# A decoder step on one core: the experts' lists of the first 256 tokens completed in three parts, one input-projection block to a head, and a number table made at the start

## The chip, the cores and the metric

The kernel runs on one core of one Trainium2 chip. The metric is the device time of one execution in microseconds (us), the median of several runs. The core has a matmul engine (PE), three engines for element-wise work (DVE, ACT, POOL), an engine that here only issues transfers (SP), and 16 DMA engines. POOL issues the indirect transfers, which fetch rows of a table by a list of numbers.

## The reference, cut to what matters

One layer is computed for 512 prompt tokens and 8 samples (one new token each), width 1024: a norm, an input projection, attention and retention, an output projection, a second norm, and then a mixer of single-neuron experts:

```
def _peer_block(xb, w_pq, sub_keys, peer_u, peer_v):
    q = (xb @ w_pq).reshape(blk, PEER_HEADS, 2, PEER_HALF)
    s = jnp.einsum('thcd,hcnd->thcn', q, sub_keys).astype(jnp.float32)
    sv, si = lax.top_k(s, PEER_TOPK)
    ...
    best, pos = lax.top_k(cand, PEER_TOPK)
    eid = jnp.take_along_axis(cidx, pos, -1)
    g = jax.nn.softmax(best, -1).astype(xb.dtype)
    u = peer_u[eid]
    a = jax.nn.gelu(jnp.einsum('thkd,td->thk', u, xb))
    return jnp.einsum('thk,thkd->td', g * a, peer_v[eid])
```

Each token has 8 heads. A head scores 2 x 128 keys, keeps the 16 best of each half, and of their sums the 16 best again. These are 16 of 16,384 experts, each a row of 1024 numbers in `peer_u` and one in `peer_v`. The layer ends in a last norm.

## The kernel before, in words

The prompt is worked on in two waves of 256 tokens, A and B; B also carries the samples. Wave A goes through attention, retention, output projection and second norm first. Then `product_keys(0, ...)` makes its lists. Head by head it projects the tokens with two blocks of `w_pq` (`project`), multiplies the result with the keys (`psco`, L846), copies the scores out of PSUM on ACT (`sc`, L850), and finds the 16 best of each half on DVE (`tk_axis`, `top16`). After each fourth head `tk_finish` completes the lists of four heads: 80 candidate sums, their 16 best, the experts' numbers `eidL` (L351) and the gates.

Between two heads runs `second`, a generator of wave B's input projection in 28 blocks of 128 columns, with B's attention and retention between them; `BLOCKS` of these blocks are done for each head.

The two waves meet the experts in different ways. Wave A and the samples *gather*. For each head and each of its 16 places, POOL issues one indirect transfer (`gather`, L929) of 128 rows of `peer_u` (128 x 1024 numbers), DVE makes the dot product (L947), and after 16 of these come 16 gathers of `peer_v` that DVE weighs and adds up (`y`, L961). There are 528 gathers: 256 for tokens 0 to 127 (`lists[0]`), 256 for tokens 128 to 255, 16 for the samples. They share 8 buffers (`GBUFS`). Wave B is *dense*: all 16,384 experts are computed for its tokens, 128 at a time, in 128 blocks ("keys"): `dense_a` (L1065, eight matmuls with a block of the turned `peer_u`), `dense_w` (L1180, times a weight that is zero for an expert not chosen) and `dense_y` (L1187, four matmuls with a block of `peer_v` that SP loads, `vt`, L1174). The weights are made by `scatter` from B's lists: it compares the lists with a table of numbers (`iota128`, `iotaE`) and multiplies on PE (L1155 to L1168). `scatter(0, n)`, 32 groups, runs ahead of the dense loop, `scatter(1, n)` inside it.

The gathers are threaded through the rest of the program by hand: `beside(g, n, per)` takes `per` gathers after each step of `g`. The numbers are in `STEPS`:

```
STEPS = (16, 7, 5, 2)
...
    step[0] += STEPS[0]
    run(work, STEPS[0])
    beside(second, 28, STEPS[1])
    inB.close()
    beside(outer(1, (catB,), hnD, None), 8, STEPS[2])
```

16 are taken at once when wave A's lists are written, 7 after each block of `second` that is left (12 of them), 5 after each of the 8 blocks of wave B's output projection (`outer(1, ...)`, which ends in the second norm and so in `hnD`, L807), 2 after each head of wave B's `product_keys(1, ...)`: 156 in all. 16 more are taken in `scatter(0)`, the others at an even pace in the dense loop and behind it. While wave B's lists are made, PE also gets `dense_a` of the first keys (`paF`).

This written order goes through a scheduler, which orders the instructions by a simulated time line; the result is one fixed queue for each engine. Each engine runs its queue in order and stands at the first instruction whose inputs are not there.

Of the kernel before, what the change touches and what calls it, by code (L numbers as in the profile page):

```python
# [9 lines left out]
F32 = mybir.dt.float32  # L10
F32R = mybir.dt.float32r
BF16 = mybir.dt.bfloat16
# [21 lines left out]
DT = 512 - GT  # L34
# [6 lines left out]
LASTA = False  # L41
CHUNKS = [0, 64, 128]
ROWS = max(b - a for a, b in zip(CHUNKS, CHUNKS[1:]))
NG = DT // 8
STEPS = (16, 7, 5, 2)
BLOCKS = 2
SOON, RATE = 16, 574
AHEAD0 = 14

# [2 lines left out]
def step_kernel(ctx, tc, x_prompt, x_sample, cache_k, cache_v, state_ret, norm1_g, w_in, ret_gn_g,  # L52
                w_out, norm2_g, w_pq, sub_keys, peer_u, peer_v, norm_f_g, u_turned, keys_turned,
                y_p, y_s, kw_p, vw_p, ret_p, kn_s, vn_s, ret_s):
    nc = tc.nc
# [8 lines left out]
    consts = ctx.enter_context(tc.tile_pool(name="consts", bufs=1))  # L64
# [24 lines left out]
    su = setup.enter_context(tc.tile_pool(name="su", bufs=1, side="right"))  # L89

    def f_iota(pool, name, p, n, pattern, base, cm):
        t = pool.tile([p, n], F32, name=name)
        nc.gpsimd.iota(t, pattern=pattern, base=base, channel_multiplier=cm,
                       allow_small_or_imprecise_dtypes=True)
        return t
# [4 lines left out]
    def ps_tile(tag, name):  # L100
        return ps.tile([128, 512], F32, name=name, tag=tag, bufs={"o": 1, "x": 1}.get(tag, 2))
# [88 lines left out]
    selT = consts.tile([128, 8], F32, name="selT")  # L190
    iota16 = consts.tile([128, TOPK], BF16, name="iota16")
    nc.vector.tensor_copy(iota16, f_iota(su, "iota16f", 128, TOPK, [[1, TOPK]], 0, 0))

    bias = fc.tile([128, 512], F32, name="bias")
    mult = fc.tile([128, 512], F32, name="mult")
# [43 lines left out]
    def tk_new(pool, name, p, heads, eid):  # L239
        d = {"p": p, "H": heads, "n": name}  # L240
        if eid:
            d["g"] = pool.tile([128, heads, TOPK], F32, name=f"g{name}")
            d["eid"] = pool.tile([128, heads, TOPK], I32, name=f"eid{name}")
        return d

    def tk_open(pool, d):
        tag = d["tmp"] + str(d["H"])
        d["val"] = pool.tile([128, d["H"], 2, TOPK], F32, name="val" + d["n"], tag="val" + tag, bufs=1)
        d["idx"] = pool.tile([128, d["H"], 2, TOPK], U32, name="idx" + d["n"], tag="idx" + tag, bufs=1)

    def lockstep(gens):

        gens = list(gens)
        while gens:
            gens = [g for g in gens if next(g, gens) is not gens]
# [13 lines left out]
    def tk_axis(pool, d, h, c, src, key):  # L269
        p = d["p"]  # L270
        return top16(pool, d["val"][:p, h, c, :], d["idx"][:p, h, c, :], src, p, NKEY, key)
# [213 lines left out]
    def retention(w, h, rqT, rkT, kdN, rvN):  # L485
# [28 lines left out]
        for T in range(2):  # L514
            cs = slice(T * 128, (T + 1) * 128)
            nc.tensor.matmul(po[:, cs], inn[:, cs], rvN[:, T, :], start=True, stop=(before[T] is None))
            if before[T] is not None:
# [9 lines left out]
                   allow_small_or_imprecise_dtypes=True)  # L527
# [296 lines left out]
    def product_keys(w, lists, listS, hn):  # L824
        qst = ExitStack()
        qp = qst.enter_context(tc.tile_pool(name="qp", bufs=2, side="right"))
        n = hn.shape[2]
        if w:
            pss = ps_tile("x", "pss")
        for d in lists:  # L830
            tk_open(qp, d)
        for hc, pas in project(w_pq2, [(hn,)], range(16)):
            hh, c = divmod(hc, 2)
            if c == 0:
                qT = qp.tile([128, 2, WT + 8], F32, name="qT")
            nc.scalar.activation(qT[:, c, :n], pas[0][:, :n], AF.Copy)  # L836
            if c == 0:
                continue
            if w:
                for c in range(2):  # L840
                    nc.tensor.matmul(pss[:, c * 64 + hh * 8:c * 64 + hh * 8 + 8], keysT[:, 2 * hh + c, :],
                                     qT[:, c, WT:], start=True, stop=True)
            pc = ps_tile("s", "psco")
            for j in range(2):
                for c in range(2):
                    nc.tensor.matmul(pc[:, (2 * j + c) * 128:(2 * j + c + 1) * 128],  # L846
                                     qT[:, c, j * 128:(j + 1) * 128], keysT[:, 2 * hh + c, :],
                                     start=True, stop=True)
            sc = qp.tile([128, 4, 128], F32, name="sc", tag="sc", bufs=SCB)
            nc.scalar.activation(sc.rearrange("p a b -> p (a b)"), pc, AF.Copy)  # L850
            lockstep(tk_axis(qp, lists[j], hh, c, sc[:, 2 * j + c, :], 2 * j + c) for j in range(2) for c in range(2))
            if hh % 4 == 3:
                lockstep(tk_finish(qp, d, hh - 3, hh + 1, LASTA or hh < 4) for d in lists)
            yield
        if w:
            sst = qp.tile([128, 128], F32, name="sst", bufs=1)
            nc.scalar.activation(sst, pss[:, :128], AF.Copy)
            psr = ps_tile("s", "psr")
            for c in range(2):
                nc.tensor.transpose(psr[:64, c * 128:(c + 1) * 128], sst[:, c * 64:(c + 1) * 64], ident)  # L860
            tk_open(qp, listS)
            ssc = qp.tile([64, 2, 128], F32, name="ssc", bufs=1)
            nc.scalar.activation(ssc.rearrange("p a b -> p (a b)"), psr[:64, :256], AF.Copy)
            lockstep(tk_axis(qp, listS, 0, c, ssc[:, c, :], c) for c in range(2))
            lockstep([tk_finish(qp, listS, 0, 1)])
            for q in range(2):
                for nm in ("eid", "g"):
                    nc.sync.dma_start(wideS[nm][q * 64:(q + 1) * 64, 0, :],
                                      listS[nm][:64, 0, q * TOPK // 2:(q + 1) * TOPK // 2])
        qst.close()  # L870


    lists = [tk_new(pD, f"L{b}", 128, PH, b < 2) for b in range(4)]
# [30 lines left out]
    def outer(w, c2, hn, outs):  # L904

        ost = ExitStack()
        op_ = ost.enter_context(tc.tile_pool(name="op", bufs=1, side="right"))
        x = op_.tile([128, 2, D], F32, name="xo")
        xs = op_.tile([8, D], F32, name="xs") if w else None
        load_x(w, x, xs)  # L910
        ssq2 = small.tile([128, 3, KB], F32, name="ssq2", tag="ssq2", bufs=1)
        nc.vector.memset(ssq2, 1.0)
        yield from out_proj(op_, c2, x, xs, ssq2)
        norm2(op_, w, x, xs, ssq2, hn)
        ost.close()
# [108 lines left out]
    def beside(g, n, per, more=None):  # L1024

        for _ in g:
            step[0] += per
            run(work, per)
            if more is not None:
                more()  # L1030

    def run(g, n=1):
        for _ in range(n):
            if g is not None:
                next(g, None)
# [8 lines left out]
    for _ in product_keys(0, lists[:2], None, hnA):  # L1044
        run(second, BLOCKS)
    nc.vector.tensor_copy(catB[:, :, WT:], catS)
# [5 lines that stand above are left out]
    mixB.close()  # L1052
# [38 lines left out]
    def early():  # L1091
        h = head[0]
        head[0] += 1
        run(first, 2 * (AHEAD0 * (h + 1) // PH - AHEAD0 * h // PH))

    beside(product_keys(1, lists[2:], listS, hnD), 8, STEPS[3], early)
    EARLY = step[0]
    front.close()

    den = ExitStack()  # L1100
    dn = den.enter_context(tc.tile_pool(name="dn", bufs=1, side="right"))
    dw = den.enter_context(tc.tile_pool(name="dw", bufs=2, side="right"))
# [2 lines left out]
    pgs = [pY.tile([128, 512], F32, name=f"pg{q}") for q in range(2)]  # L1105
    paT, pgt = ring[0], pgs[0]
    yps = [[pY.tile([128, 512], F32, name=f"y{b}{q}") for q in range(2)] for b in range(2)]
    iota128f = dw.tile([128, DT], F32, name="iota128f", tag="lgt")[:, :128]
    nc.gpsimd.iota(iota128f, pattern=[[1, 128]], base=0, channel_multiplier=0, allow_small_or_imprecise_dtypes=True)
    iota128 = dn.tile([128, 128, 8], BF16, name="iota128")  # L1110
    nc.vector.tensor_copy(iota128, iota128f[:, :, None].to_broadcast([128, 128, 8]))

    iotaE = dn.tile([128, 16, 8], BF16, name="iotaE")
    nc.vector.tensor_copy(iotaE, iota128f.rearrange("p (a b) -> p a b", b=8))

    l5 = dn.tile([128, 5, DT], BF16, name="l5")
    lJ, lI, lg3 = l5[:, 0], l5[:, 1], l5[:, 2:]
# [187 lines left out]
```

## Time and profile before

| what | value |
|---|---|
| median of 3 runs | 1716.3 us (1715.61 to 1717.32) |
| profiled execution, its own time | 1717.34 us |
| span of the profile | 1715.6 us |
| PE busy | 1522.8 us, 89% |
| DVE busy | 1188.2 us, 69% |
| POOL busy | 772.7 us, 45% |
| ACT busy | 415.7 us, 24% |
| moved by DMA | 507.14 MB |

The profiled execution's own time is 1.7 us above the span: what lies outside the first and the last instruction. Durations below are of this one execution. "Busy" leaves out register, semaphore and DMA-issuing instructions. PE shows two records for each of these f32 matmuls.

### The profile page before, as it was taken

What the parts mean: (1) busy time and instruction counts of PE and PEld (TensorE: products, weight loads), DVE (VectorE), ACT (ScalarE), POOL (GpSimd) and SP (SyncE); (2) the same over time, 40 slices, a digit from 0 to 9 for tenths busy, and PEclk for the clock granted to TensorE, in tenths of its full rate; (3) what the DMA queues carried; (4) which work ended last, traced back from release to release, by engine and by line L of the source; (5) the groups of instructions that cost most, each with busy time, mean ns of one, the idle gap of its engine ahead of it and who ended that gap; (6) DMA issues with size and microseconds to landing.
All of it is one profiled execution on the core that took longest, in us unless ns stands there. A gap on an engine that the chain in (4) does not pass through costs nothing.

```text
span 1715.6 us, 21739 instructions
## 1 busy us (share of the span) xinstructions
PE 1522.8 (89%) x7544; PEld 1117.8 (65%) x7544; DVE 1188.2 (69%) x2869; ACT 415.7 (24%) x846; POOL 772.7 (45%) x656
## 2 busy tenths in 40 slices
PE   5987789998764698996799999999999999999995
PEld 5975647876653487886566667667676666666642
DVE  5667614597998699979997666566556555555666
ACT  5743623342212311326411112111110000000001
POOL 2155330035567674105764544444454544544552
PEclk9988899998886799995699999999999999999998
DMA  6577674379999999553599989999998999999996
GB/s 197 154 205 221 196 213 143 107 234 361 325 350 362 344 364 350 172 197 102 173 405 405 355 325 367 332 334 343 344 339 333 392 357 372 353 358 360 332 409 238
DMA packets 213517, 507.14 MB, mean 296 GB/s; under 512 B 16552, under 2 KB 103128, under 8 KB 213280
## 3 DMA queue, kind: packets, MB, share of 16 engines
q0 software_dynamic: 81952, 295.80, 47.2%
q1 hardware_dynamic: 131456, 209.95, 35.5%
q8 instruction: 60, 0.98, 0.2%
q14 instruction: 49, 0.40, 0.1%
HBM read 495.82 MB, written 9.86 MB: 295 GB/s over the span
## 4 chain that ended last, share of the span: by engine, by line
PE 32%; issue 26%; DVE 16%; POOL 10%; DMA 7%; ACT 2%; POOLq 0%; SPq 0%; DVEq 0%; ACTq 0%
PE pa L1065 8%; PE y L1187 8%; PE pa L157 8%; POOL v L929 5%; POOL u L929 4%; DVE y L961 3%; DVE u L947 3%; PE pg L1166 2%; DMA v<-in_peer_v,eidL 2%; DMA raw<-in_w_out 2%; DVE oi L1160 1%; DMA raw<-in_w_pq 1%; DMA kv<-in_cache_v_win 1%; DVE oj L1155 1%; PE paF L1065 1%
## 5 line engine op out<-in xcount | busy, mean ns | idle before, releaser
L929 POOL DMA_INDIRECT u<-in_peer_u,eidL x256 | 331.5, 1295 | 379.6 <-PE pT L452 113.2
L929 POOL DMA_INDIRECT v<-in_peer_v,eidL x256 | 331.2, 1294 | 303.4 <-DVE a L947 123.0
L1187 PE MATMUL y<-vt,ge 128*128 128x512 f32 x1024 | 460.5, 596 | 7.5 <-DVE y L961 7.5
L1065 PE MATMUL pa<-hnD,ut 128*128 128x256 f32 x1792 | 410.2, 382 | 4.8 <-ACT ge L1069 4.8
L1065 PEld LDWEIGHTS pa<-hnD,ut 128*128 128x128 f32 x1792 | 340.6, 192 | 81.5 <-issue 34.9
L961 DVE SCALAR_TENSOR_TENSOR y<-v,gw,y 128x1024 f32<-128x1024 f32 x261 | 336.1, 1288 | 19.8 <-DMA v<-in_peer_v,eidL 11.2
L1187 PEld LDWEIGHTS y<-vt,ge 128*128 128x128 f32 x1024 | 195.6, 191 | 209.8 <-issue 203.7
L947 DVE CUSTOM_DVE_ANT_0 u<-u,hq 128x1024 f32<-128x1024 f32 x264 | 313.6, 1217 | 9.0 <-DMA u<-in_peer_u,eidL 9.0
L1180 DVE TENSOR_TENSOR ge<-ge,big 128x256 f32<-128x256 f32 x128 | 52.0, 423 | 197.3 <-ACT ge L1069 183.4
L1069 ACT ACTIVATE ge<-pa 128x256 f32<-128x256 f32 x112 | 42.9, 383 | 502.8 <-PE pa L1065 400.8
L157 PE MATMUL pa<-hnD,raw 128*128 128x256 f32 (+1 forms) x512 | 128.3, 403 | 10.6 <-DMA raw<-in_w_pq 8.1
L1166 PEld LDWEIGHTS <-oj 128*128 128x128 bf16 x1536 | 100.1, 167 | 42.5 <-DVE oi L1160 25.4
L157 PEld LDWEIGHTS pa<-hnD,raw 128*128 128x128 f32 x512 | 101.2, 202 | 35.7 <-issue 11.2
L1155 DVE TENSOR_TENSOR oj<-iota,l 128x1024 bf16<-128x1024 bf16 x64 | 44.0, 687 | 100.8 <-PE pg L1166 92.0
L157 PE MATMUL pa<-xTB,raw 128*128 128x256 f32 x448 | 106.1, 390 | 1.3 <-DMA raw<-in_w_in 1.3
L157 PEld LDWEIGHTS pa<-xTB,raw 128*128 128x128 f32 x448 | 85.5, 197 | 14.1 <-ACT qT L836 0.9
L1168 ACT ACTIVATE big<-pg 128x512 f32<-128x512 f32 x48 | 53.2, 1109 | 152.5 <-PE pg L1166 130.9
L1166 PE MATMUL pg<-oi,oj 128*128 128x64 bf16 x1152 | 75.9, 230 | 14.7 <-DVE oi L1160 13.6
L126 PE MATMUL pa<-xT,wh 128*128 128x264 f32 x224 | 70.4, 315 | 8.7 <-ACT xT L119 4.4
L127 PE MATMUL pa<-xT,wh 128*128 128x264 f32 x224 | 68.3, 305 | 0.1
L128 PE MATMUL pa<-xT,wl 128*128 128x264 f32 x224 | 67.6, 302 | 0.6 <-DVE wl L120 0.6
L1160 DVE TENSOR_TENSOR oi<-oi,lx 128x1536 bf16<-128x1536 bf16 x64 | 60.3, 950 | 0.0
(515 smaller groups left out, 1720.4 us busy)
## 6 DMA issues: line engine op xcount, KB each, us to landing
ut<-in_u_turned SPq DMA_DIRECT2D x128, 512.0 KB
vt<-in_peer_v SPq DMA_DIRECT2D x128, 512.0 KB
raw<-in_w_in SPq DMA_DIRECT2D x56, 512.0 KB
raw<-in_w_pq SPq DMA_DIRECT2D x16, 1024.0 KB
raw<-in_w_out SPq DMA_DIRECT2D x8, 1024.0 KB
kv<-in_cache_k_win POOLq DMA_DIRECT2D x24, 256.0 KB
kv<-in_cache_v_win POOLq DMA_DIRECT2D x24, 256.0 KB
u<-in_peer_u,eidL POOLq DMA_INDIRECT x256
```

Source lines behind the costliest of these rows:

```text
L126: nc.tensor.matmul(out, wh, xh, start=first, stop=False)
L127: nc.tensor.matmul(out, wh, xl, start=False, stop=False)
L128: nc.tensor.matmul(out, wl, xh, start=False, stop=last)
L157: nc.tensor.matmul(pa[:, :n], part[:, k, :], x[0][:, k, :], start=(k == 0), stop=(k == KB - 1))
L929: nc.gpsimd.indirect_dma_start(out=t[:p], out_offset=None, in_=tab, in_offset=bass.IndirectOffsetOnAxis(ap=d["eid"][:p, h, k:k + 1], axis=0))
L947: nc.vector.tensor_tensor_reduce(out=u[:p], in0=u[:p], in1=hn, scale=1.0, scalar=0.0, op0=OP.mult, op1=OP.add, accum_out=a[:, k:k + 1])
L961: nc.vector.scalar_tensor_tensor(y, v[:p], w[:, k:k + 1], y, op0=OP.mult, op1=OP.add)
L1065: nc.tensor.matmul(pa, ut[:, k, :], hnD[:, k, :DT], start=(k == 0), stop=(k == KB - 1))
L1155: nc.vector.tensor_tensor(out=oj, in0=iota128, in1=lJ[:, None, ts].to_broadcast([128, 128, 8]), op=OP.is_equal)
L1160: marks[c] = nc.vector.tensor_tensor(out=oi3, in0=oi[:, None].to_broadcast([128, 3, ne, 64]), in1=lx[:, 1:, None].to_broadcast([128, 3, ne ...
L1166: nc.tensor.matmul(pg_[:, t * ni:(t + 1) * ni], oj[:, :, t], oi3[:, z, :, es], start=(z == 0), stop=(z == 2))
L1187: nc.tensor.matmul(yps[b][q], ge[:, b * 128:(b + 1) * 128], vt[:, q * 512:(q + 1) * 512], start=(i == 0), stop=(i == NKEY - 1))
```

## The change

Four things change. `STEPS` and `BLOCKS`: one block of `second` to a head in place of two, so that 20 blocks are left behind wave A's lists in place of 12, with 5 gathers to a block in place of 7; ahead of `product_keys(1)`'s end stand 16 + 100 + 40 + 16 = 172 gathers in place of 156. `ENDS`: the lists of wave A are completed after heads 1, 3 and 7 (heads 0 and 1, 2 and 3, 4 to 7) in place of 3 and 7; those of wave B as before. The number table: 128 numbers in bf16 are made among the constants, and the den stage copies from them.

```
-STEPS = (16, 7, 5, 2)
-BLOCKS = 2
+STEPS = (16, 5, 5, 2)
+BLOCKS = 1
+ENDS = ((1, 3, 7), (3, 7))
...
+    iota128b = consts.tile([128, 128], BF16, name="iota128b")
+    nc.vector.tensor_copy(iota128b, f_iota(su, "iota128f", 128, 128, [[1, 128]], 0, 0))
...
-            if hh % 4 == 3:
-                lockstep(tk_finish(qp, d, hh - 3, hh + 1, LASTA or hh < 4) for d in lists)
+            if hh in ENDS[w]:
+                h0 = max([0] + [e + 1 for e in ENDS[w] if e < hh])
+                lockstep(tk_finish(qp, d, h0, hh + 1, LASTA or hh < 4) for d in lists)
...
-    iota128f = dw.tile([128, DT], F32, name="iota128f", tag="lgt")[:, :128]
-    nc.gpsimd.iota(iota128f, pattern=[[1, 128]], base=0, channel_multiplier=0, allow_small_or_imprecise_dtypes=True)
     iota128 = dn.tile([128, 128, 8], BF16, name="iota128")
-    nc.vector.tensor_copy(iota128, iota128f[:, :, None].to_broadcast([128, 128, 8]))
-
-    iotaE = dn.tile([128, 16, 8], BF16, name="iotaE")
-    nc.vector.tensor_copy(iotaE, iota128f.rearrange("p (a b) -> p a b", b=8))
+    nc.vector.tensor_copy(iota128, iota128b[:, :, None].to_broadcast([128, 128, 8]))
+
+    iotaE = iota128b.rearrange("p (a b) -> p a b", b=8)
```

The scheduler makes new queues of this. Three places follow; in the changed kernel the line numbers are 3 to 4 higher up to the den stage and 1 higher behind it.

DVE's queue before, at the first dot product (L947). `eidL_296` and `eidL_298` are the experts' numbers of the first and second 128 tokens, and 128x64 is four heads of 16:

```order
L345 TENSOR_TENSOR pick_3430<-eq 128x64
L343 TENSOR_TENSOR eq<-eq 128x64x8
L351 SCALAR_TENSOR_TENSOR eidL_296<-pick_3410,pick_3430 128x64
...
L351 SCALAR_TENSOR_TENSOR eidL_298<-pick_3412,pick_3432 128x64
L448 RECIPROCAL rs<-sm 128x1
L947 ISA u,a<-u,hq 128x1024
L947 ISA a 128x1
L258 MAX valL_2807<-sc 128x8 x2
```

The same place of the changed kernel; 128x32 is two heads of 16:

```order
L354 SCALAR_TENSOR_TENSOR eidL_300<-pick_3021,pick_3041 128x32
L261 MAX valL_2811<-sc 128x8 x2
L261 MAX valL_2813<-sc 128x8 x2
...
L354 SCALAR_TENSOR_TENSOR eidL_302<-pick_3023,pick_3043 128x32
L444 ISA lg,nm<-psc,bh 128x384
L444 ISA nm 128x1
L269 MAX_INDEX idxL_2812<-valL_2811,rest 128x8
L951 ISA u,a<-u,hq 128x1024
```

The first dot product stood behind the lists of heads 0 to 3; it now stands behind those of heads 0 and 1. From there to the rows that write `hnD` at the end of wave B's second norm, DVE's queue held 108 to 110 dots and sums, and now holds 152 to 154. The two completions of wave A's lists held 198 DVE instructions, the three now hold 254.

PE's queue before, at the last heads of wave B's lists (`pa<-hnD,raw` is the projection with `w_pq`, `paF` is `dense_a` of the first keys, `psco` a head's scores):

```order
L157 MATMUL pa<-hnD,raw 128x264 x16
L1065 MATMUL paF<-hnD,ut 128x256 x16
L841 MATMUL pss<-qT,keysT 128x8 x2
L846 MATMUL psco<-keysT,qT 128x128
L1065 MATMUL paF<-hnD,ut 128x256 x8
L846 MATMUL psco<-keysT,qT 128x128 x3
L860 MATMUL psr<-ident,sst 64x128 x2
L1065 MATMUL paF<-hnD,ut 128x256 x48
```

The same place of the changed kernel:

```order
L1069 MATMUL paF<-hnD,ut 128x256 x15
L158 MATMUL pa<-hnD,raw 128x264 x16
L1069 MATMUL paF<-hnD,ut 128x256 x3
L844 MATMUL pss<-qT,keysT 128x8
L849 MATMUL psco<-keysT,qT 128x128
L1069 MATMUL paF<-hnD,ut 128x256 x6
L844 MATMUL pss<-qT,keysT 128x8
L849 MATMUL psco<-keysT,qT 128x128 x3
L1069 MATMUL paF<-hnD,ut 128x256 x7
```

Ahead of the last head's first `psco` PE's queue held 64 `paF` matmuls between the heads, and now holds 105. In `scatter(0)` it held groups of 21, 12 and 4 `dense_a` matmuls between the scatter's own, and now holds none there; the dense loop behind it is unchanged. On DVE, the stretch of wave B's lists held 45 dots and sums, and now holds 17.

SP's queue before, at the program's end (`hx` is the rows to which the samples' sum is added, `xb` those of wave B):

```order
L1174 DMA vt<-in_peer_v 128x1024 x15
L966 DMA hx<-hs 8x1024
L982 DMA out<-y 128x1024
L1174 DMA vt<-in_peer_v 128x1024 x5
L1253 DMA xb<-hs 128x1024 x2
L982 DMA out<-y 8x1024
L1269 DMA out<-xb 128x512 x4
```

The same place of the changed kernel:

```order
L1175 DMA vt<-in_peer_v 128x1024 x10
L970 DMA hx<-hs 8x1024
L986 DMA out<-y 128x1024
L1175 DMA vt<-in_peer_v 128x1024 x6
L1254 DMA xb<-hs 128x1024 x2
L1175 DMA vt<-in_peer_v 128x1024
L986 DMA out<-y 8x1024
L1175 DMA vt<-in_peer_v 128x1024 x3
L1270 DMA out<-xb 128x512 x4
```

The load of `hx` stood five `vt` loads before the last one, and now stands ten before it. PE's matmul that adds up the samples (`selT`, two halves) stood one key before the end of PE's queue, and now stands eight keys before it. Behind DVE's last `dense_w` stood 42 gathers, and now stand 27. On POOL, the `iota` of the den stage stood behind the first 163 gathers and is gone there.

## Rows read from the trace of the kernel before

**Rows 1.** Stretches: busy us of each engine, granted PE clock, DMA share, GB/s.

```profile
300.00:364.00 64.00, 64.00 (x347) 52.41 (x346) 44.97 (x257) 28.09 (x60) 0.00 (x0) 1.00 0.41 117
364.00:598.00 234.00, 156.94 (x726) 126.43 (x725) 196.88 (x531) 57.45 (x141) 147.96 (x117) 0.82 0.97 345
598.00:706.00 108.00, 102.03 (x475) 87.85 (x475) 105.50 (x407) 23.66 (x49) 60.20 (x48) 0.94 0.92 332
706.00:746.00 40.00, 35.22 (x157) 30.36 (x156) 37.77 (x216) 11.32 (x23) 0.00 (x0) 0.91 0.37 119
746.00:842.00 96.00, 72.38 (x895) 67.89 (x893) 85.34 (x144) 51.01 (x79) 50.52 (x17) 0.67 0.45 149
842.00:1620.00 778.00, 778.00 (x3285) 527.85 (x3283) 484.78 (x709) 93.53 (x182) 385.95 (x316) 1.00 0.95 355
1620.00:1716.00 96.00, 76.62 (x173) 32.57 (x171) 65.64 (x82) 11.18 (x22) 39.80 (x34) 0.92 0.82 322
```

**Rows 2.** Timeline of DVE: at the first gather, and at wave B's second norm.

```profile
363.02 0.21 DVE L351 SCALAR_TENSOR_TENSOR eidL<-pick,pick 128x64 int32<-128x64 f32 x1
368.91 1.25 DVE L947 CUSTOM_DVE_ANT_0 u<-u,hq 128x1024 f32<-128x1024 f32 x1 [3.31 <-DMA u<-in_peer_u,eidL]
...
601.00 0.86 DVE L807 TENSOR_SCALAR hnD<-pt,gT 128x256 f32<-128x256 f32 x2
```

**Rows 3.** Timeline of ACT: scores of wave A's heads 1 and 3, wave B's head 7.

```profile
287.66 0.58 ACT L850 ACTIVATE sc<-psco 128x512 f32<-128x512 f32 x1
329.65 0.59 ACT L850 ACTIVATE sc<-psco 128x512 f32<-128x512 f32 x1
707.27 0.60 ACT L850 ACTIVATE sc<-psco 128x512 f32<-128x512 f32 x1 [0.28 <-PE psco L846]
```

**Rows 4.** Timeline of POOL: the first gather, and the number table.

```profile
364.18 1.08 POOL L929 DMA_INDIRECT u<-in_peer_u,eidL  x1 [113.16 <-PE pT L452]
747.42 0.24 POOL L1109 IOTA iota128f<- 128x128 f32 x1 [50.61 <-DVE eidS L351]
```

**Rows 5.** DMA queues, 300 to 364 us: packets, MB, share of 16 engines.

```profile
q1 hardware_dynamic: 11058, 7.44, 40.3%
```

**Rows 6.** DMA queues, 364 to 598 us.

```profile
q0 software_dynamic: 16248, 59.20, 68.0%
q1 hardware_dynamic: 26798, 21.46, 29.1%
```

**Rows 7.** DVE's groups by shape, 364 to 598 us: busy, mean ns, idle before.

```profile
L947 DVE CUSTOM_DVE_ANT_0 u<-u,hq 128x1024 f32<-128x1024 f32 x64 | 76.7, 1216 | 6.8 <-DMA u<-in_peer_u,eidL 6.8
L961 DVE SCALAR_TENSOR_TENSOR y<-v,gw,y 128x1024 f32<-128x1024 f32 x45 | 59.4, 1320 | 0.3
L947 DVE DVE_READ_ACCUMULATOR2_ANT a<- 128x1 f32 x64 | 5.0, 79 | 0.0
```

**Rows 8.** A stretch of the dense loop, columns as in the first group.

```profile
875.00:900.00 25.00, 25.00 (x116) 16.73 (x115) 22.41 (x29) 3.20 (x7) 18.28 (x15) 1.00 1.03 409
```

**Rows 9.** PE's groups by shape, 598 to 706 us.

```profile
L1065 PE MATMUL paF<-hnD,ut 128*128 128x256 f32 x127 | 28.9, 379 | 0.0
```

**Rows 10.** Timeline of DVE: the number table and the scatter.

```profile
747.69 0.69 DVE L1111 CAST iota<-iota128f 128x1024 bf16<-128x1024 f32 x1 [0.43 <-POOL iota128f L1109]
751.87 0.69 DVE L1155 TENSOR_TENSOR oj<-iota,l 128x1024 bf16<-128x1024 bf16 x1 [3.35 <-ACT l L1125]
762.06 0.69 DVE L1155 TENSOR_TENSOR oj<-iota,l 128x1024 bf16<-128x1024 bf16 x1 [2.51 <-PE pg L1166]
770.18 0.69 DVE L1155 TENSOR_TENSOR oj<-iota,l 128x1024 bf16<-128x1024 bf16 x1 [3.22 <-PE y L1166]
```

**Rows 11.** Timelines of DVE, PE and SP's queue at the program's end.

```profile
1693.35 1.28 DVE L961 SCALAR_TENSOR_TENSOR y<-v,gw,y 128x1024 f32<-128x1024 f32 x1 [0.43 <-DMA v<-in_peer_v,eidW]
1682.51 16.21 PE L1187 MATMUL y<-vt,ge 128*128 128x512 f32 x32 [7.54 <-DVE y L961]
1673.05 0.29 SPq L966 DMA_DIRECT2D hx<-hs  x1
```

## The prediction

> **What bounds the kernel now.** I read the stretches first, cut where the work changes [rows 1]. From 300 to 364 us PE is busy throughout, at the full granted clock: wave A's lists with blocks of wave B's input projection between them. From 364 to 598 us PE works 157 of 234 us, and the DMA engines are at 97% with 345 GB/s: gathers, and wave B's weights. Up to 706 us PE is the bound again (102 of 108), with DVE full beside it (105.5). From 706 to 746 us DVE completes wave B's lists, to 842 us it makes the scatter (85 of 96), and from there to 1620 us PE is busy without a gap at full clock. Behind that come 96 us in which the gathers that are left end.
>
> Then I looked for what opens each stretch. Wave A's head 3 has its scores on ACT at 329.65 us [rows 3], DVE writes the experts' numbers of heads 0 to 3 at 363.02, POOL issues the first gather at 364.18 [rows 4], and DVE makes the first dot product at 368.91 after 3.31 us of waiting for the transfer [rows 2]. The stretch that follows ends when DVE has written `hnD` (601.00 us the last row of it), because everything from PE's `product_keys(1)` on needs that. DVE's queue is in order, so `hnD` cannot be written before the dots and sums that stand ahead of it, and those not before their rows have landed.
>
> **The change part by part.** *First gather.* The lists now start with heads 0 and 1. Head 1's scores come at 287.66 us, and about 284 without one of the two blocks that stood ahead of them. Behind the scores of head 3 stand 34 us to the first gather, for four heads' completion; for two I take two thirds, 22. The gathers start near 305 us in place of 364.
>
> *Front end.* This is the large term. Ahead of `hnD` 152 to 154 gathers must now be consumed where it was 108 to 110: 45 more, against a start that is 59 us earlier. What a gather costs: 59.20 MB of the indirect queue [rows 6] are 113 landed gathers of 0.524 MB. So some 157 must land, 82.3 MB, and beside them what the hardware queue moved from 300 us on, 7.44 MB [rows 5] and 21.46 MB [rows 6], and 1 MB that I add for what is cut off at the ends: 112.2 MB. At the 345 GB/s that this mix had with the engines full, that is 325 us: from 305 to 630. The other way, by the engines' own time: a gather took 0.68 of 234 us over 113, 1.41 us, so 157 take 221; the loads took 68.1 us (29.1% of 234), 25.8 us (40.3% of 64) and some 3 us for the added 1 MB. That is 318 us, at 97% 328: 633. DVE sets the other bound. A dot with its read-out, or a sum, costs (76.7 + 5.0 + 59.4) / 109 = 1.29 us [rows 7]; 154 of them make 199 us, the other work of DVE in the two stretches was 45.0 + 55.8, and 56 more instructions for the third completion cost 0.2 us each by the 128x64 row at 363.02 [rows 2], 11 us. Together 311: not before 616 us if DVE never stood, and, at the 84% that it reached from 364 to 598, 370 us and 675. I take 635, just above the transfers' bound since DVE will stand for some of them, where before it was 601: **+34**, with ends at +15 (DVE without a gap) and +55.
>
> The Trainium skill bears on this ("DMA: Bandwidth & Descriptors", "Where 436 GB/s comes from"): it says that between HBM and SBUF the HBM side, about 358 GB/s, binds below the fabric's 435. By that figure the 112.2 MB would take an estimated 313 us and the front end would be at 618. The trace doesn't agree that it is a limit: one stretch of the dense loop shows 409 GB/s [rows 8].
>
> *Wave B's lists.* Ahead of the last head's scores PE has 41 more `paF` matmuls. 127 records are 64 matmuls in 28.9 us [rows 9], 0.45 us each: 18.5 us. Against it, PE's 6 us of idle time in this stretch [rows 1] mostly go, since DVE has 17 dots and sums there where it had 45, some 36 us less by the row price. **+14**, from +8 to +20. It isn't work added: those matmuls are missing later, in the scatter, where they cost little. From the last scores (707.27 us [rows 3]) DVE needed 39 us to complete the lists; it no longer enters that stretch behind, **-4** (0 to -6).
>
> *Scatter and table.* In `scatter(0)` DVE waited 2.51 and 3.22 us for PE's products behind `dense_a` groups [rows 10]; those groups are gone: **-5** (0 to -8). Of the number table, `iota` on POOL [rows 4] made DVE wait 0.43 us, and one small cast goes; the new one at the start stands ahead of everything, beside the first loads. POOL stood 50.61 us at its `iota`, with the gathers behind it, but that is hidden: the 8 buffers were full before, and at 751.87 DVE waits for ACT's lists, 3.35 us, not for a transfer. **0** to -1.
>
> *Dense loop.* PE has the same matmuls there, and no gap to lose: **0**.
>
> *End.* Behind the last `dense_w` 27 gathers are left, where 42 took from 1621 to 1693 us [rows 11], 1.73 us each: the last lands some 26 us sooner after the loop. PE waited 7.54 us at 1682, behind the samples' sum (DVE's `y`), while SP stood at `hx` until 1673 with five `vt` loads queued behind it. Now the samples' matmul stands eight keys before PE's end. A key is eight records, so the 16.21 us of the 32 records are four keys, and eight take 32 us. PE, with 77 us of work in this stretch, comes to the samples' matmul 45 us after 1620, about when 27 gathers are through (47 us and a short chain). So most of the wait goes, and 0 to 6 us may come back at the new place: **-7** (-9 to -3).
>
> The sum is +34 + 14 - 4 - 5 - 0.5 - 7 = +31.5, on the profiled execution's 1717.3: 1749. The median of the runs shown is 1 us lower, so 1748.
>
> **Rivals.** *The transfers go faster* (the other side): at the 409 GB/s of [rows 8], 112.2 MB take 274 us, the front end comes at 579, which is 22 us earlier than before, and with the other terms (-2.5) the kernel takes about 1692. DVE's bound of 616 speaks against the whole of it, as does 97% of the engines' time at 345 GB/s; the 409 stand for a short part of the dense loop, whose mean is 355. It decides from a front end of 603 us down, which needs 377 GB/s. Chance 0.06.
>
> *No change.* The front end reaches DVE's and the transfers' bounds together (605 to 610), and PE's 41 matmuls fill its gaps for nothing: 1714 to 1720. For it speaks that the gathers now start beside a stretch with the DMA at 41%; against it that PE was full there and the sum already counts that room. Chance 0.05.
>
> *DVE becomes the bound.* The dots come in among wave A's top-16 work, each waiting for a transfer while the chain behind it feeds the next list: DVE stays at 84%, the front end is at 675, +74, and the kernel near 1788. Against it: at its dots it stood only 6.8 us in 234 before [rows 7]. Chance 0.09.
>
> *The table is worth something.* If POOL's 50 us at `iota` had held gathers that DVE wanted, their going would give up to 8 x 1.4, 11 us. It would show as DVE waiting for rows at 750, and it doesn't. It only shifts the forecast: 1737. Chance 0.05, within the forecast's range.
>
> **How the numbers follow.** The forecast has 0.75 with a range of its own from the ends of the terms: front end +15 to +55, others together between -12 and +8 (not all at one end): 1722 to 1772. With 0.05 for the table inside that range, it holds the 8 in 10; the rest lies at both sides. A measurement of this kernel can tell about 0.2% (3.4 us) from no change. Faster: the first rival and a little of the second, 0.07. Same: 0.04. Slower: 0.89.
>
> **What would show it.** The first indirect transfer near 305 us. From there to the end of the second norm the DMA share at 95% or more, and PE idle for longer than the 77 us of before. The first `product_keys(1)` matmul near 632, where it was 598. The last scores of wave B near 755 (707 before), the first `dense_y` near 880 (842), then an unchanged 778 us. In the end, PE's stop at `dense_y` gone, or a stop of a few us at the samples' matmul. The prediction is wrong if the front end comes below 610 us: if transfers in 305 to 364 go beside PE's work at a rate that no stretch of before shows, or if DVE's dots there fit into waits that I have counted as work. It is too low if DVE stands at rows while POOL waits for a buffer, in turn, since then neither bound is reached.

## The result, and the profile after

The changed kernel takes 1747.7 us (median of 4 runs, 1744.21 to 1748.46), against 1716.3 us before: a ratio of 1.0178, with a 95% interval of 1.0158 to 1.0197. The forecast was 1748. Its profiled execution has a span of 1746.2 us.

The stretches of the changed kernel, cut at the same places of the program as [rows 1] (columns as there):

```profile
302.00:640.00 338.00, 234.12 (x1079) 187.65 (x1078) 288.34 (x840) 95.63 (x213) 203.91 (x159) 0.81 0.94 329
640.00:754.00 114.00, 114.00 (x563) 99.93 (x563) 77.54 (x370) 25.71 (x55) 31.79 (x22) 0.99 0.61 212
754.00:790.00 36.00, 33.47 (x150) 28.55 (x149) 32.98 (x201) 11.06 (x22) 0.00 (x0) 0.95 0.41 132
790.00:883.00 93.00, 61.76 (x823) 55.54 (x822) 91.69 (x161) 50.86 (x76) 37.47 (x20) 0.56 0.45 141
883.00:1661.00 778.00, 778.00 (x3284) 527.71 (x3283) 483.78 (x691) 92.87 (x181) 389.28 (x313) 1.00 0.96 354
1661.00:1746.00 85.00, 71.49 (x161) 30.02 (x159) 42.29 (x63) 11.03 (x21) 19.79 (x18) 0.93 0.66 253
```

The dense loop is as it was: 778 us, PE full, full clock. All the loss lies ahead of it; the end is 5 us shorter than before. The landmarks, from the timelines of the changed kernel by tile (first and last start of each; the first row is POOL's first gather):

```profile
302.51 1.04 POOL L933 DMA_INDIRECT u<-in_peer_u,eidL  x1 [52.13 <-DVE eq L346]
L810 DVE TENSOR_SCALAR hnD<-pt,gT x8: 472/483/486, 236.8 to 641.3; 128x256 f32<-128x256 f32 x8
L158 PE MATMUL pa<-hnD,raw x210: 386/386/647, 640.2 to 719.8; 128*128 128x264 f32 x105
L853 ACT ACTIVATE sc<-psco x16: 578/597/604, 268.2 to 754.3; 128x512 f32<-128x512 f32 x16
L1156 DVE TENSOR_TENSOR oj<-iota,l x64: 676/691/737, 793.1 to 1318.8; 128x1024 bf16<-128x1024 bf16 x64
L1188 PE MATMUL y<-vt,ge x1024: 592/592/1222, 876.7 to 1736.8; 128*128 128x512 f32 x171
L1181 DVE TENSOR_TENSOR ge<-ge,big x128: 409/424/474, 875.1 to 1656.4; 128x256 f32<-128x256 f32 x128
```

The first gather comes at 302.5 us where it was at 364.2 [rows 4], and yet `hnD` is ready 40 us later, 641.3 against 601.0 [rows 2]. The last scores are at 754.3 (707.3 [rows 3]), and the first `dense_y` at 876.7, where the loop of before began at 842 [rows 1].

DVE's groups from 302 to 640 us, and the DMA queues there (columns as in [rows 6, 7]):

```profile
L951 DVE CUSTOM_DVE_ANT_0 u<-u,hq 128x1024 f32<-128x1024 f32 x90 | 108.3, 1217 | 9.2 <-DMA u<-in_peer_u,eidL 8.7 <-issue 0.5
L965 DVE SCALAR_TENSOR_TENSOR y<-v,gw,y 128x1024 f32<-128x1024 f32 x63 | 80.5, 1278 | 1.6 <-DMA v<-in_peer_v,eidL 1.3
L951 DVE DVE_READ_ACCUMULATOR2_ANT a<- 128x1 f32 x89 | 7.3, 83 | 0.0
```

```profile
q0 software_dynamic: 22490, 81.91, 66.2%
q1 hardware_dynamic: 39168, 29.04, 27.7%
```

153 dots and sums and 111 MB, as counted ahead (154 and 112.2). But the waits for their rows are only 11 us in 338. That is a first sign that the front end is not set where I put it: had the gathered rows come too late, DVE would stand at its dots. It is no more than a sign, since transfers can also hold up PE, which stands 31 us for loads of weights in this stretch.

In the tail PE no longer stands at `dense_y`, and does stand, for 4.94 us, at the samples' sum (timeline of PE):

```profile
1705.49 3.57 PE L1012 MATMUL pa<-y,selT 128*8 128x512 f32 x4 [4.94 <-DVE y L965]
```

### The profile page after: what moved, and what is told of

Same layout as the page of the kernel before. It is cut to its first block, busy times and chain, and to the rows that moved or that the text cites. A ratio compares the mean times of both kernels' runs of the same rounds, so it can differ in the third digit from the quotient of the medians.

```text
span 1746.2 us, 21797 instructions
## 1 busy us (share of the span) xinstructions
PE 1529.6 (88%) x7544; PEld 1122.2 (64%) x7544; DVE 1192.7 (68%) x2925; ACT 425.7 (24%) x862; POOL 771.4 (44%) x656
## 4 chain that ended last, share of the span: by engine, by line
PE 64%; DVE 12%; DMA 10%; issue 5%; ACT 2%; POOL 1%; SPq 0%; DVEq 0%; POOLq 0%; ACTq 0%
PE y L1188 23%; PE pa L1069 22%; PE pa L158 10%; DMA raw<-in_w_pq 3%; PE pg L1167 3%; PE paF L1069 3%; DVE u L951 2%; DVE y L965 2%; DVE oi L1161 2%; DMA raw<-in_w_out 1%; DVE oj L1156 1%; DMA u<-in_peer_u,eidL 1%; DMA kv<-in_cache_v_win 1%; DMA v<-in_peer_v,eidW 1%; DMA raw<-in_w_in 1%
## 5 line engine op out<-in xcount | busy, mean ns | idle before, releaser
L933 POOL DMA_INDIRECT u<-in_peer_u,eidL x256 | 335.9, 1312 | 454.8 <-DVE y L965 205.3
L933 POOL DMA_INDIRECT v<-in_peer_v,eidL x256 | 324.8, 1269 | 293.7 <-DVE y L965 117.9
L951 DVE CUSTOM_DVE_ANT_0 u<-u,hq 128x1024 f32<-128x1024 f32 x264 | 317.3, 1226 | 19.3 <-DMA u<-in_peer_u,eidL 16.1
L158 PE MATMUL pa<-hnD,raw 128*128 128x256 f32 (+1 forms) x512 | 131.8, 416 | 21.7 <-DMA raw<-in_w_pq 21.7
L158 PEld LDWEIGHTS pa<-hnD,raw 128*128 128x128 f32 x512 | 105.0, 209 | 46.4 <-DMA raw<-in_w_pq 23.3
```

The source lines that it names most:

```text
L158: nc.tensor.matmul(pa[:, :n], part[:, k, :], x[0][:, k, :], start=(k == 0), stop=(k == KB - 1))
L933: nc.gpsimd.indirect_dma_start(out=t[:p], out_offset=None, in_=tab, in_offset=bass.IndirectOffsetOnAxis(ap=d["eid"][:p, h, k:k + 1], axis=0))
L951: nc.vector.tensor_tensor_reduce(out=u[:p], in0=u[:p], in1=hn, scale=1.0, scalar=0.0, op0=OP.mult, op1=OP.add, accum_out=a[:, k:k + 1])
```

## The experiments

The kernel before was run again beside each group; there its runs spread from 1707 to 1726 us, so ratios are given, each against the kernel before beside it. One profile of the same kernel can differ from the next by 11 us in the front end (the table alone: `hnD` read by PE at 597.5 and at 608.4 us in two profiles), so that single profiles are used for differences of 20 us and more, or for the length of a stretch.

**The parts alone.** Each is the changed kernel with the other parts as before.

The number table alone:

```
-STEPS = (16, 5, 5, 2)
-BLOCKS = 1
-ENDS = ((1, 3, 7), (3, 7))
+STEPS = (16, 7, 5, 2)
+BLOCKS = 2
+ENDS = ((3, 7), (3, 7))
```

> The changed kernel with steps, blocks and lists as before: only the number table is made at the start. By my reading its cost was hidden: 1715 to 1717 us, DVE still waiting for ACT's lists at the first comparison of the scatter. Rival, that POOL's 50 us at its iota held back gathers: 1705 to 1711.

Measured: ratio 0.9966 (0.9952 to 0.998). It stands against my reading, but its profile has every landmark within 2.2 us of before, first `dense_y` at 841.4, and behind the table DVE still waits for ACT's lists (timeline of DVE):

```profile
751.27 1.29 DVE L1156 TENSOR_TENSOR oj<-iota,l 128x1024 bf16<-128x1024 bf16 x2 [4.19 <-ACT l L1126]
```

So it was run once more, and oftener:

> The number table alone once more, with more rounds, since the first time its ratio was 0.9966 while every stage of its profile began within 2 us of before. By my reading nothing on the path changed: a ratio of 0.998 to 1.001. Rival, that the table is worth its 0.3%: 0.995 to 0.998.

Measured: 0.9997 (0.9976 to 1.0017). The first gain did not come back, and no row of the profile carries it. The table is worth nothing that can be told here; POOL's 50 us at the `iota` [rows 4] were indeed hidden.

The lists in three parts alone (and the table):

```
-STEPS = (16, 5, 5, 2)
-BLOCKS = 1
+STEPS = (16, 7, 5, 2)
+BLOCKS = 2
```

> The lists of wave A in three parts (and the table), but two blocks to a head and 7 gathers to a block as before. DVE's queue then holds 136 to 138 dots and sums ahead of hnD (110 before, 153 changed). If the number of gathers ahead of hnD against their start sets the front end: first gather near 306, 140 gathers and the loads are some 102 MB, at 345 GB/s 297 us, hnD at 603 to 615, the kernel 1718 to 1730. Rival, that one block to a head does the harm: hnD at 590 to 600, 1705 to 1714.

Measured: ratio 1.0046 (1.0024 to 1.0067); first gather 308.5 us, PE's first matmul with `hnD` at 603.3. As expected by the number of gathers: 28 more of them ahead of `hnD` took up all of a 56 us earlier start.

One block to a head alone (and the table):

```
-ENDS = ((1, 3, 7), (3, 7))
+ENDS = ((3, 7), (3, 7))
```

> One block to a head and 5 gathers to each of 20 blocks, lists of wave A in two parts as before (and the table). DVE's queue holds 106 to 108 dots and sums ahead of hnD, as before, and the lists come four blocks earlier (first gather near 350). If the gathers ahead of hnD set the front end: hnD at 585 to 600, the kernel 1702 to 1716. Rival, that the order of the blocks does the harm: hnD at 635 or later, 1740 and more.

Measured: ratio 0.9999 (0.9979 to 1.002), first gather 353.1 us, PE's first `hnD` matmul at 592.7. With the lists as late as before, the order of the blocks does no harm. (What the front end and wave B's lists win here, 6 and 14 us in the profile, is lost behind them: the first comparison comes 74.5 us after the last scores, in place of 44.6. DVE has 64 dots and sums between `hnD` and that place, where it had 46.) So no part alone costs what the change does (0.5% and nothing, against 1.8%): the two together put 153 gathers ahead of `hnD`, each alone 137 and 107.

**The number of gathers.** The changed kernel with all its parts, but with the gathers of wave B's lists held behind the last `hnD` instruction of DVE, and fewer before:

```
-STEPS = (16, 5, 5, 2)
+STEPS = (16, 3, 4, 6)
...
-            run(work, per)
+            if holds:
+                with tc.issue_after(holds[-1].ins):
+                    run(work, per)
+            else:
+                run(work, per)
```

> The changed kernel with 3 gathers to a block, 4 to an output-projection block and 6 to a head of wave B's lists, these last held behind the last hnD instruction on DVE: 112 dots and sums ahead of hnD in place of 153, 155 at the end of wave B's lists, all else as changed (lists in three parts, one block to a head). If the gathers ahead of hnD set the front end: 115 of them and the loads are 90 MB, 261 us at 345 GB/s, so that PE's and DVE's own work bounds it: hnD at 575 to 600, the kernel 1690 to 1712. Rival, that the third completion and the dots among the lists make DVE the bound whatever their number: hnD at 620 or later, 1725 and more.

Measured: ratio 1.001 (0.9988 to 1.0032). With 112 ahead in place of 153 the whole loss is gone. The timeline of PE by tile:

```profile
L158 PE MATMUL pa<-hnD,raw x256: 386/386/808, 600.1 to 703.8; 128*128 128x264 f32 x128
```

`hnD` is there 40 us sooner than in the changed kernel for 41 gathers less. But it is no sooner than before the change, and the 1690 to 1712 us that I expected are not reached. What holds it there is seen in its stretches:

```profile
301.00:560.00 259.00, 195.00 (x929) 157.23 (x927) 226.59 (x738) 78.14 (x148) 153.20 (x115) 0.86 0.92 319
560.00:600.00 40.00, 32.78 (x148) 26.43 (x149) 9.76 (x27) 16.30 (x63) 1.46 (x1) 0.84 0.52 173
```

Up to 560 us DVE is at 87% and the DMA engines at 92%; then come 40 us of output projection and norm in which neither has much to do. DVE's queue and the transfers were both still possible as the bound here.

**Transfers or DVE.** Two kernels take one from the other. In the first, half of the first 160 gathers are left out, and every second dot or sum reads the rows of the one before:

```
-                u = gather(u_tab, d, h, k, "u")
+                cut[0] += 1
+                if cut[0] > 160 or k % 2 == 0:
+                    t_ = gather(u_tab, d, h, k, "u")
+                u = t_
```

(the same for `v`, and `STEPS = (16, 5, 5, 0)`, so that the number ahead of `hnD` stays at 155).

> The changed kernel with half of its first 160 gathers left out: every second dot or sum reads the rows fetched for the one before it, so that its result is not the reference's. DVE's queue holds 155 dots and sums ahead of hnD (153 changed), but only about 78 are fetched: 71 MB with the loads. If the transfers set the front end, it falls to DVE's own work and PE's, hnD at 605 to 625 (640 changed), the kernel 1715 to 1733. Rival, that DVE's queue sets it whatever is fetched: hnD at 635 to 645, 1742 to 1752.

Measured: 1754.1 us, ratio 1.0212 (1.0183 to 1.0241): not faster than the changed kernel. PE's first `hnD` matmul:

```profile
L158 PE MATMUL pa<-hnD,raw x208: 386/386/647, 642.7 to 715.1; 128*128 128x264 f32 x104
```

The indirect queue moves 44.57 MB there in place of 81.91, the DMA share falls to 67%, and `hnD` comes at 642.7, where the changed kernel has 640.2. So fewer transfers alone do not bring it sooner. But the scheduler made another order of this kernel, and that has to be seen before anything follows. The output projection opens when PE has turned the last rows of wave B's retention (`py<-yo`; the last start counts), here for the kernel before, the changed one and this one:

```profile
L482 PE MATMUL py<-ident,yo x8: 421/434/449, 466.8 to 533.5; 128*128 128x128 f32 x8
L485 PE MATMUL py<-ident,yo x8: 421/434/447, 517.7 to 576.3; 128*128 128x128 f32 x8
L485 PE MATMUL py<-ident,yo x8: 421/433/448, 497.1 to 600.5; 128*128 128x128 f32 x8
```

The stretches of the three from 300 us to that place:

```profile
300.00:533.50 233.50, 184.19 (x921) 150.60 (x920) 197.36 (x713) 67.58 (x134) 105.24 (x85) 0.89 0.82 280
300.00:576.30 276.30, 199.56 (x938) 161.12 (x936) 247.13 (x781) 78.42 (x149) 162.91 (x130) 0.83 0.94 322
300.00:600.50 300.50, 190.96 (x943) 154.24 (x943) 283.90 (x831) 78.06 (x151) 119.95 (x85) 0.82 0.68 221
```

With half the transfers all 155 dots and sums stand ahead of that place, 31 more than in the changed kernel, and it comes 24 us later, with DVE busy 94% of the time. Behind it `hnD` takes 42 us in place of 64: no gather runs beside the output projection there, and PE waits 1.4 us for its weights (`w_out`) where it waited 12.2. So the run shows that DVE's queue, nearly full and with half the transfers gone, comes to the same 640 us by itself. It does not show that the transfers cost nothing: they take 22 us less in the second part, which the other order gives back in the first.

In the second, the same rows are fetched whole, and DVE works on half of their columns:

```
+                m = 512 if cut[0] <= 160 else D
-                nc.vector.tensor_tensor_reduce(out=u[:p], in0=u[:p], in1=hn, scale=1.0, scalar=0.0,
+                nc.vector.tensor_tensor_reduce(out=u[:p, :m], in0=u[:p, :m], in1=hn[:, :m], scale=1.0, scalar=0.0,
```

(the sums likewise).

> The changed kernel with the first 160 dots and sums done over half of the columns, so that its result is not the reference's; every row is still fetched whole. DVE's queue holds 145 of them ahead of hnD, and each takes some 0.6 us less: 85 us of DVE's work go. If the transfers set the front end: 148 gathers and the loads are 107.5 MB, 311 us at 345 GB/s, hnD at 613 to 630. Rival, that DVE sets it: hnD at 590 to 602, where the kernel of before has it.

Measured: ratio 1.002 (0.9991 to 1.0048), 27 us less than the changed kernel. DVE's dots from 305 to 608 us, the whole stretch, and PE's first `hnD` matmul:

```profile
L955 DVE CUSTOM_DVE_ANT_0 u<-u,hq 128x512 f32<-128x512 f32 x80 | 53.6, 683 | 17.5 <-DMA u<-in_peer_u,eidL 17.1 <-issue 0.3
```

```profile
305.00:608.00 303.00, 226.39 (x1073) 179.88 (x1072) 206.49 (x821) 94.41 (x212) 164.32 (x151) 0.88 0.98 350
```

```profile
L158 PE MATMUL pa<-hnD,raw x253: 386/386/647, 609.5 to 720.0; 128*128 128x264 f32 x127
```

With DVE 82 us shorter (288.3 to 206.5), `hnD` comes 31 us sooner and no more, because now the transfers are the bound: 98% at 350 GB/s, and DVE stands at its dots for 17.5 us. Some 10 of the 31 us are an estimate for the 8 dots and sums that this order has fewer ahead of `hnD` (145 in place of 153, at 1.29 us). Neither number of the two theories came out whole: the first expected 605 to 625 with half the transfers and got 642.7, and the second expected 590 to 602 here, without the transfers close behind.

**Where the 42 us lie.** The same cut in all the runs, at PE's last `py` (dots and sums counted by their start in the timeline of DVE; us):

| run | dots and sums ahead of it | DVE busy, from 300 us to it | last `py` | from it to PE's first `hnD` matmul | dots and sums in between |
|---|---|---|---|---|---|
| before | 79 | 197 of 234 | 533.5 | 64.7 | 32 |
| changed | 124 | 247 of 276 | 576.3 | 63.9 | 31 |
| lists alone | 107 | 225 of 237 | 536.6 | 66.7 | 32 |
| blocks alone | 77 | 198 of 226 | 526.1 | 66.6 | 32 |
| 112 ahead | 107 | 228 of 259 | 559.3 | 40.8 | 1 |
| half the transfers | 155 | 284 of 301 | 600.5 | 42.2 | 0 |
| half of the columns on DVE | 113 | 182 of 248 | 547.6 | 61.9 | 32 |

The whole loss of the front end stands in the first part, where DVE has 45 more dots and sums ahead and is busy 50 us longer; the second part has the same length before and after. Against the kernel before, the run with 112 wins 24 us in the second part, where hardly a gather is left, and loses 26 in the first, where they now stand: that is why it is no sooner than before. One thing stays open. The lists alone and the run with 112 have the same 107 ahead, and yet lie 23 us apart: DVE idles 11 us in the one and 32 in the other, which has one block to a head. The changed kernel has 29. What one block to a head costs when the lists come early was not tested by itself.

**The matmuls among wave B's lists.** `AHEAD0 = 9` in place of 14 in the changed kernel:

> The changed kernel with 9 blocks of dense_a ahead of the scatter in place of 14: PE has 65 paF matmuls ahead of wave B's last scores where the changed kernel has 105, the rest moves to the scatter; hnD as changed. By my term of 0.45 us for each matmul, the last scores come 12 to 18 us earlier after hnD (114 changed, 96 to 102 here), and the scatter with PE at 62 of 93 us takes most of them back for nothing: 1733 to 1742. Rival, that the place of these matmuls makes no difference because PE is short of time all the way to the first dense_y: 1745 to 1750.

Measured: ratio 1.0129 (1.0105 to 1.0154), where the changed kernel has 1.0178. With 65 `paF` matmuls in place of 105, the last scores come 98.8 us after PE's first `hnD` matmul (645.6 to 744.4), where it was 114.1: 0.38 us for each of the 40 matmuls that moved. From the first comparison to the first `dense_y` it takes 91.0 us in place of 83.6. The scatter takes half of it back, where I had said it would cost little.

**A version from the parts.** The experiments suggest what helps: an early start that is spent on no more than about 140 gathers ahead of `hnD`, and then, since DVE has fewer dots left among wave B's lists, fewer `dense_a` matmuls there. Three kernels with the lists in three parts, two blocks to a head, and less `dense_a` ahead:

```
-STEPS = (16, 5, 5, 2)
-BLOCKS = 1
+STEPS = (16, 7, 5, 4)
+BLOCKS = 2
-AHEAD0 = 14
+AHEAD0 = 9
```

> A candidate: lists in three parts, two blocks to a head, steps 16, 7, 5 and 4 (139 gathers ahead of hnD, 171 at the end of wave B's lists, 27 left behind the last dense_w) and 9 blocks of dense_a ahead. With the front end at 603 as in the run with the lists alone, wave B's lists 8 to 15 us shorter by the 40 matmuls that move to the scatter, and a tail of 80 us as changed in place of 88: 1698 to 1712. Rival, that the scatter takes the matmuls' time in full and DVE's 16 more dots fill the gap: 1713 to 1722.

Measured: 1716.5 us, ratio 0.998 (0.9964 to 0.9997), in the rival's range. With `STEPS = (16, 7, 5, 2)`, that is 16 gathers fewer among wave B's lists:

> A candidate: lists in three parts, two blocks to a head, steps 16, 7, 5 and 2 as before, 9 blocks of dense_a ahead in place of 14. DVE has 137 to 139 dots and sums ahead of hnD and only 16 behind it in wave B's lists, PE has 65 paF matmuls there: hnD at 603 to 608, last scores 97 to 101 us later, first comparison 39 later, scatter 91, so the first dense_y at 832 to 838 (842 before), a tail as before: 1705 to 1713, ratio 0.993 to 0.998. Rival, that the scatter takes what the lists give: first dense_y at 840 or later, ratio 0.999 or more.

Measured: 1711.0 us, ratio 0.9966 (0.9944 to 0.9987), first `dense_y` at 838.9. This is the fastest of all, 2% under the changed kernel. Its third of a per cent against the kernel before is not secured: the table alone had the same ratio the first time, with an interval below 1 as well, and it did not come back. With `AHEAD0 = 6`:

> The same with 6 blocks of dense_a ahead: 48 paF matmuls ahead of the last scores. Wave B's lists 7 us shorter again if PE still bounds them (90 to 94 us), the scatter 0 to 5 us longer: ratio 0.991 to 0.997. Rival, that DVE or the loads of w_pq bound the lists by then: no shorter than with 9, and the scatter longer: 0.997 to 1.001.

Measured: ratio 0.9988 (0.997 to 1.0007). First `dense_y` at 836.7, only 2 us sooner; the lists came 96 us after PE's first `hnD` matmul, against 99 with 9 blocks. This goes the rival's way. Which engine bounds the lists by then is not shown: PE is still busy 92.5 of 96 us there, and stands 3.4 us for a load of `w_pq`.

## Why the prediction was right, and where it was not

The time was met to 1 us, and the terms add up to it only in sum. The measured ones are differences between the landmarks of the two profiles.

**First gather**, 305 us: 302.5. The reckoning by the second head's scores was right.

**Front end**, +34 with `hnD` at 635: +40 to +42, with `hnD` at 641. The size was near and the cause was named wrong. I held the transfers for the bound (630 to 633) and DVE for the second (616 without a gap). With half of the rows fetched `hnD` came no sooner, in the order that this made; with DVE's dots and sums halved it came 31 us sooner. The rival "DVE becomes the bound" was the nearest: DVE's share stayed at 85% (288.3 of 338 us), just as it had been 84%. I gave that 0.09, and its price came out too high, at 675. The error in that price is DVE's other work: 112 us in my sum, while the stretch shows 288.3 less 196.1 for dots and sums, 92 us. With the measured 92 the same rule gives (196 + 92) / 0.84 = 343 us from 302.5, 645 us. The argument that I used against it, that DVE had stood only 6.8 us at its dots [rows 7], in truth spoke for it: an engine that does not wait for rows is not held up by them. The reason that the rival gave, dots that each wait for a transfer, was wrong too: DVE stood 9.2 us at its dots in the changed kernel.

**Why DVE is not full.** Two things are seen. Up to the last `py` DVE idles 29 us in the changed kernel, 6 of them for rows and 22 for results of ACT and PE; PE waits 19 us for weights of wave A's lists there, in place of 6 before, so the loads have a part in it whose size no run separates. Behind that come the output projection and the norm, a chain over PE, ACT and DVE in which DVE is busy for 43 of 64 us with the gathers in it, and for 8 of 42 us in the run with half the transfers, where they are gone.

**Wave B's lists**, +14: +5 (109 us from PE's first `hnD` matmul to the last scores before, 114 now). The row price of the `paF` matmuls was right: 28.9 us before [rows 9], 47.7 now, 18.8 more where I had 18.5. PE's 6 us of idle time went wholly, as PE had 114 of 114 us busy. The term that was left out is PE's other work, which is the same matmuls in less time (PE's groups by shape, 598 to 706 us before, 640 to 754 now):

```profile
L157 PE MATMUL pa<-hnD,raw 128*128 128x264 f32 x256 | 64.0, 412 | 3.1 <-DMA raw<-in_w_pq 2.5 <-issue 0.7
L158 PE MATMUL pa<-hnD,raw 128*128 128x264 f32 x256 | 59.9, 390 | 0.0
L1069 PE MATMUL paF<-hnD,ut 128*128 128x256 f32 x210 | 47.7, 380 | 0.0
```

With the scores' matmuls, up to the last of them, that is 5.5 us less. Before, PE stood 2.5 us for a load at 672 and 2.8 us for ACT at 684, and its granted clock was 0.50, the lower of its two levels, from 685 to 690; the changed kernel's PE has no gap there and 0.99 in the whole stretch, where it was 0.94 [rows 1]. The 2 us that are left are records that overlap more. The same holds against the run with 9 blocks: its 0.38 us for a matmul that moved is less than 0.45, since its projection takes 61.0 us, and a wait of 1.0 us for a load comes back.

**Completion**, -4: from the last scores to the first comparison 38.8 us in place of 44.6, -6. **Scatter**, -5: 83.6 in place of 90.1, -6.5. **Table**, 0 to -1: nothing, by two runs. **Loop**, 0: +1. These held.

**End**, -7: from the last `dense_w` (1620.5 us before, 1656.4 now) to the span's end 95 us before and 90 now, -5. The stop of 7.54 us at `dense_y` went [rows 11], and one of 4.94 us came at the samples' sum, inside the 0 to 6 us that were named.

Together +42 + 5 - 6 - 6.5 + 1 - 5 = +30.5, the difference of the two spans. The front end came out 8 us above my term and wave B's lists 9 us below, and the two cancelled; that the sum is off by 1 us is in part luck.

**The rule of the Trainium skill** ("DMA: Bandwidth & Descriptors", "Where 436 GB/s comes from") gave an estimated 618 us for the front end by 358 GB/s. In the one run in which the transfers bound it, they did so at a mean of 350 GB/s and 98% of the engines' time, with `hnD` at 609.5 for 145 gathers. That mean is near the Trainium skill's figure, but the trace does not show it as a limit: from the last `py` to `hnD`, the same run moved 394 GB/s for 62 us.

## What to carry to other kernels

An earlier start of a stream of work is worth nothing if the instructions that open the next stage stand behind more of that stream in an engine's queue: count how many stand ahead of them before and after, and multiply by the engine's own price. When two resources are both nearly full, look at which of them is waited for: DVE's 11 us of waiting at 153 transfers spoke against the transfers as the bound, while their 94% share, against DVE's 85%, suggested it. When an experiment takes work away, look at the order that the scheduler makes of what is left, before the time is read: with half the transfers 31 dots and sums changed their place. And edits that each do little alone can cost when together: the same numbers in `STEPS` and `BLOCKS` put 107 gathers ahead of `hnD` with late lists and 153 with early ones.

## What the runs showed that I had not expected

Leaving out half of the gathered rows, 37 MB less in 338 us, brought no time, with the DMA share falling from 94% to 67%. A share of 94% did not mean that the transfers set the time: what the kernel had to move in it happened to need nearly all of it.

The scheduler's order hardly follows the written number of gathers for each step: with the same 156 written ahead of wave B's lists, DVE's queue holds 107 or 153 of them ahead of `hnD`, depending on when the lists come. The edge behind an instruction, in the run with 112, together with smaller numbers, capped it.
